# Input projection of a two-layer hybrid trunk: four of eight K pairs per chunk pair with seven block products, in two phases on four accumulators

## The chip, the cores and the metric

The kernel runs on one core of one Trainium2 chip. The metric is the device time of one execution in microseconds (us), the median of several runs. Engines are named as in the profile: PE (TensorE), DVE (VectorE), ACT (ScalarE), POOL (GpSimd), SP (SyncE, which here only issues DMAs).

## The reference

Two layers on x of 256 tokens by 2048 columns, in float32:

```python
for l in range(DEPTH):                                   # 2
    h = rms_norm(x, pre_mix_norm[l])
    proj = h @ w_in[l]                                   # 2048 x 6144
    # q_sb, k_sb, v_sb, q_d, k_d, v_d: six groups of 1024 columns, 8 heads each
    o_sb = rms_norm(stick_breaking_attention(q_sb, k_sb, v_sb), sb_out_norm[l])
    o_d = rms_norm(differential_attention(rope(q_d), rope(k_d), v_d, lam), diff_subln[l]) * (1 - lam_init)
    m = concat(o_sb, o_d) @ w_o[l]                       # 2048 x 2048
    x = x + rms_norm(m, post_mix_norm[l])
    h = rms_norm(x, pre_ffn_norm[l])
    x = x + rms_norm((silu(h @ w_gate[l]) * (h @ w_up[l])) @ w_down[l], post_ffn_norm[l])   # 5632 wide
```

## The kernel before

**Numbers.** A float32 matrix product is made of three matmuls. Each operand is split into `hi` (the value rounded to the PE's float32r format, made by ACT) and `lo` (the rest, made by DVE as value minus `hi`). `product` adds hi·hi, hi·lo and lo·hi into one PSUM accumulator of 128 tokens by 512 columns.

**Tiles.** K is taken in pairs of 128 rows ("K pair", eight of them for 2048), columns in chunks of 512, tokens in two halves. The twelve chunks of the input projection come in six pairs (`PAIRS`), numbered n = 0 to 5; four accumulators hold a chunk pair (2 token halves x 2 chunks). A plain K pair is eight products (`eight_in`): 2 rows of K x 2 token halves x 2 chunks.

**Seven products.** For some K pairs the 2x2x2 block product is done in Winograd's form with seven products (`seven_products`). The weight blocks of such a K pair are g (first chunk, rows 0 and 1) and u (second chunk, rows 0 and 1). Besides g0 and g1 the form needs five mixed blocks: t1, t2, t3, t4 and b22 (`mixed_weights`), and sums of token blocks (`pair_forms`, `token_sums`: `sh`, `sl`). Three or four of the seven products go to sums of their own (p1, p6, p7, q5), which are combined later (`shared_part`) and added when the accumulators are read.

**Input projection before** (`mixer_in`). Pair 0 is plain. In pairs 1 to 4, K pairs 4 and 5 have seven products, in the order `IN_ORDER`, with p1, p6, p7 and q5 in four extra PSUM banks; while these are taken, `burst` and `clear` keep attention out, which uses the same banks. After the second one `shared_part` reads the four banks (one ACT copy, four DVE operations), and `settle` adds the result to each of the four accumulators on DVE before ACT scales it. Pair 5 has no extra banks free: `sevens_alone` runs K pairs 4 and 5 first, in the four accumulators themselves, copies them out on ACT in between (`kept_part`), puts a plain K pair between, and three DVE operations combine the copies; `settle` then needs three additions (`added_alone`). The output projection starts with `sevens_alone` as well.

**Weights.** All weights lie in DRAM in the order in which they are used (`weight_order`, `weights_laid_out`), 512 KB a tile of two K rows by one chunk. `fetch` issues their loads on SP into four `raw` buffers, or for the sevens of this stage into four `late` rooms, shared with other stages (`GU`). The sum of the first row's blocks, t1, is made for most sevens of this stage by an accumulating DMA from POOL into SBUF (`added`). `feed` splits tiles in order into six `hi` and six `lo` buffers, four tiles ahead of the one in use (`LOOKAHEAD`); sevens hold their other mixed blocks in buffers of their own (`Th`, `Tl`).

**Attention.** It runs as generators beside the projection, moved on by `tick`, which is called once for each two products or so. A chunk pair's queries and keys are transposed (`flip`) some ticks behind the pair's end, 3 and 6 for the stick-breaking heads and 21 and 24 for the differential heads:

```python
            wait = 3
            for c in cc:
                if c // 2 not in (2, 5):
                    start(flip(c, toks), wait if c // 2 < 3 else wait + 18)
                    wait += 3
```

`diff_weights` then makes scores, softmax maps (`s_df`, `mx_df`, `e_df`) and their transposes, `stick_weights` the stick-breaking weights (`a_sb`, `ah_sb`), `attend` and `norm_pair` the heads' outputs. The order on each engine is fixed when the program is built.

Of the kernel before, what the change touches and what calls it, by code (L numbers as in the profile page):

```python
# [83 lines left out]
def in_order(n):  # L84

    if n == 0:
        return tuple(range(KT // 2))
    return IN_LAST if n == len(PAIRS) - 1 else IN_ORDER


def weight_order():
# [3 lines left out]
    def queue_pair(name, l, kp, c):  # L95
        order.append((name, l, kp, c))
        return len(order) - 1

    plan = []
    sevens, plain, own, added, aside = set(), set(), set(), set(), {}  # L100
    for l in range(L):
        lay = {"in": {}, "o": {}, "gate": {}, "up": {}, "down": {}}
        for n, (ca, cb) in enumerate(PAIRS):
            for kp in in_order(n):
                lay["in"][ca, kp] = queue_pair("w_in", l, kp, ca)
                lay["in"][cb, kp] = queue_pair("w_in", l, kp, cb)
                if kp in IN_NOW[n]:
                    plain.add(lay["in"][cb, kp])
                    if n > 1 or l:
                        added.add(lay["in"][cb, kp])  # L110
        aside[lay["in"][PAIRS[-1][1], IN_LAST[1]]] = "v"
        order_o = [(c, kp) for kp in KP_O for c in (0, 1)]
        order_o += [(c, kp) for kp in LATE_O for c in (2, 3)] + [(c, kp) for c in (2, 3) for kp in LAST_O]
        lay["order_o"] = order_o
        for c, kp in order_o:
# [3 lines left out]
            if c == 1 and kp in KP_O[:2]:  # L119
                plain.add(lay["o"][c, kp])  # L120
        aside[lay["o"][1, KP_O[1]]] = "sums"
# [16 lines left out]
    return order, plan, sevens, plain, own, added, aside  # L138


def weights_laid_out(inputs):

    import numpy as np

    order = weight_order()[0]
    out = np.empty((len(order), P, 2 * CW), np.float32)
    for o, (name, l, kp, c) in zip(out, order):
        w = inputs[name][l, kp * 2 * P : (kp + 1) * 2 * P, c * CW : (c + 1) * CW]
        o[...] = w.reshape(2, P, CW).transpose(1, 0, 2).reshape(P, 2 * CW)
    return out  # L150
# [36 lines left out]
def kernel(  # L187
# [35 lines left out]
    order, plan, sevens, plain, own, added, aside = weight_order()  # L223
# [8 lines left out]

    ready = {}
    raws, loads = [], []
    fed = [0]

    def fetch(upto):
        while len(raws) < min(upto, len(stream)):
# [7 lines left out]
            if i + 1 in sevens:  # L246
# [4 lines left out]
                continue  # L251
            if i in own or i + 1 in own:
                raw = mix_pool[0].tile([P, 2, CW], F32, tag="v", bufs=2, name=f"V{i}")
            elif i in plain or i + 1 in plain:
                raw = late_room([P, 2, CW], f"GU{i}")
            else:
                raw = wpool.tile([P, 2, CW], F32, tag="raw", bufs=4, name=f"raw{i}")
            mixing = bool({i, i + 1} & (own | plain))
            with not_ahead(i) if mixing else nullcontext():
                loads.append(nc.sync.dma_start(raw, stream[i]))  # L260
            raws.append(raw)
            if not mixing:
                usual.append((i, loads[-1]))
            elif i in added:
                nc.gpsimd.dma_start(raw[:, 0, :], stream[i - 1][:, 0, :], accum_op=ALU.add)
# [16 lines left out]
    heads_pool = [None]  # L282
    mix_raw = [None, 0, 0, 0]

    def mixed_weights(i):
# [4 lines left out]
        if i in own or i in aside:  # L290
            th = wpool.tile([P, 2, CW], F32R, tag="hi", bufs=6, name=f"Th{i}")
            tl = wpool.tile([P, 2, CW], F32R, tag="lo", bufs=6, name=f"Tl{i}")
        if i in own:
            th2 = mix_pool[0].tile([P, 2 * (S + P)], F32R, tag="ah", bufs=1, name=f"T2h{i}")[:, 0:CW]
            tl2 = mix_pool[0].tile([P, 2 * (S + P)], F32R, tag="al", bufs=1, name=f"T2l{i}")[:, 0:CW]
        elif i in aside:
            if aside[i] == "v":
                both = heads_pool[0].tile([P, 2, CW], F32R, tag="v", bufs=2, name=f"T2{i}")
                th2, tl2 = both[:, 0, :], both[:, 1, :]
            else:  # L300
                th2, tl2 = (
                    mix_pool[0].tile([P, 4, P], F32R, tag=tag, bufs=len(IN_SEVEN), name=f"T2{tag}{i}").rearrange("p j c -> p (j c)")
                    for tag in ("sh", "sl")
                )
        else:
            th = mix_pool[0].tile([P, 3, CW], F32R, tag="Th", bufs=1 if i in plain else 2, name=f"Th{i}")
# [1437 lines left out]
```

## Time and profile before

| | |
|---|---|
| median of 3 runs | 2175.76 us (2175.2 to 2175.97) |
| span of the profiled execution | 2174.5 us |
| PE busy, idle | 2161.7 us (99%), 12.8 us |
| DVE busy | 1941.0 us (89%) |
| ACT busy | 1413.9 us (65%) |
| granted TensorE clock | 1.000 |
| DMA | 475.16 MB, 219 GB/s |
| input projection, layer 0, pairs 0 to 5 end near | 47, 93, 142, 190, 240, 293 us |
| input projection, layer 1, pairs 0 to 5 end near | 1129, 1175, 1224, 1272, 1321, 1374 us |

The profile is of one execution, whose own time is its span; the median of the runs is 1.3 us longer. A line of a group has the line of kernel.py, the engine, the operation, what it writes and reads, shapes, the count, busy time and mean length, and the engine's idle time just before with what ended it. Matmul rows overlap: each is 0.39 us long, and the next one starts before it ends. The pairs' ends are read from the first reading of an accumulator behind each pair (the `w<-in,w` additions and the `tok` and `v` scalings).

### The profile page before, as it was taken

What the parts mean: (1) busy time and instruction counts of PE and PEld (TensorE: products, weight loads), DVE (VectorE), ACT (ScalarE), POOL (GpSimd) and SP (SyncE); (2) the same over time, 40 slices, a digit from 0 to 9 for tenths busy, and PEclk for the clock granted to TensorE, in tenths of its full rate; (3) what the DMA queues carried; (4) which work ended last, traced back from release to release, by engine and by line L of the source; (5) the groups of instructions that cost most, each with busy time, mean ns of one, the idle gap of its engine ahead of it and who ended that gap; (6) DMA issues with size and microseconds to landing.
All of it is one profiled execution on the core that took longest, in us unless ns stands there. A gap on an engine that the chain in (4) does not pass through costs nothing. (4 is left out here: it accounts for less than half of the span.)

```text
span 2174.5 us, 28797 instructions
## 1 busy us (share of the span) xinstructions
PE 2161.7 (99%) x9932; PEld 1781.1 (82%) x9932; DVE 1941.0 (89%) x2627; ACT 1413.9 (65%) x2113; POOL 261.7 (12%) x256
## 2 busy tenths in 40 slices
PE   9999999999999999999999999999999999999998
PEld 7888888888888888888888888888888888888886
DVE  7887878899999999999878888788999999999997
ACT  7666765765766666666566667757566666676664
POOL 1110000022221220000011100000212212200000
PEclk9999999999999999999999999999999999999999
DMA  9556446497887776777475564455978878767683
GB/s 331 188 184 219 161 170 202 156 305 235 245 259 225 232 234 224 234 226 256 149 252 184 198 207 166 165 184 182 293 237 255 253 226 237 234 214 246 202 269 99
DMA packets 142867, 475.16 MB, mean 219 GB/s; under 512 B 16240, under 2 KB 17264, under 8 KB 142208
## 3 DMA queue, kind: packets, MB, share of 16 engines
q1 hardware_dynamic: 121952, 436.03, 58.1%
q0 software_dynamic: 20192, 36.74, 10.1%
q8 instruction: 78, 1.28, 0.2%
q14 instruction: 69, 0.57, 0.1%
q10 hardware_dynamic: 576, 0.54, 0.1%
HBM read 464.86 MB, written 8.39 MB: 218 GB/s over the span
## 5 line engine op out<-in xcount | busy, mean ns | idle before, releaser
L349 DVE TENSOR_TENSOR lo<-raw,hi 128x1024 fp32r<-128x1024 f32 x442 | 535.3, 1230 | 77.8 <-ACT hi L339 77.0
L339 ACT ACTIVATE hi<-raw 128x1024 fp32r<-128x1024 f32 x464 | 475.1, 1056 | 74.6 <-PE in L1214 28.0
L1269 PE MATMUL c<-hi,xF 128*128 128x512 f32 x1344 | 364.4, 392 | 0.5 <-DVE xF L546 0.5
L1269 PEld LDWEIGHTS c<-hi,xF 128*128 128x128 f32 x1344 | 249.8, 188 | 53.0 <-ACT act L1479 1.6
L279 POOL DMA_DIRECT2D T<-in_weights_in_turn_dram x122 | 107.2, 879 | 1223.7 <-DMA T<-in_weights_in_turn_dram 311.9
L1269 PE MATMUL c<-lo,xF 128*128 128x512 f32 x672 | 207.4, 390 | 0.0
L311 ACT ACTIVATE Th<-T 128x512 fp32r<-128x512 f32 x122 | 77.2, 633 | 199.0 <-DVE T L322 196.0
L311 ACT ACTIVATE Th<-G 128x1024 fp32r<-128x1024 f32 x122 | 129.0, 1058 | 79.7 <-DVE G L323 78.3
L1592 PE MATMUL dn<-hi,jh 128*128 128x512 f32 x416 | 162.0, 389 | 0.0
L1593 PE MATMUL dn<-lo,jh 128*128 128x512 f32 x416 | 161.8, 389 | 0.0
L313 DVE TENSOR_TENSOR Tl<-G,Th 128x1024 fp32r<-128x1024 f32 x122 | 148.9, 1221 | 11.6 <-ACT Th L311 11.6
L339 ACT ACTIVATE hi<-G 128x1024 fp32r<-128x1024 f32 x122 | 128.8, 1056 | 36.6 <-DMA G<-in_weights_in_turn_dram 22.5
L313 DVE TENSOR_TENSOR lo<-T,hi 128x1024 fp32r<-128x1024 f32 x122 | 152.3, 1248 | 0.1
L323 DVE TENSOR_TENSOR G<-G,T 128x1024 f32<-128x1024 f32 x122 | 148.7, 1218 | 1.9
L1269 PEld LDWEIGHTS c<-lo,xF 128*128 128x128 f32 x672 | 126.0, 188 | 26.5
L349 DVE TENSOR_TENSOR lo<-G,hi 128x1024 fp32r<-128x1024 f32 x104 | 126.8, 1219 | 10.0 <-ACT hi L339 9.8
L311 ACT ACTIVATE hi<-T 128x1024 fp32r<-128x1024 f32 x122 | 128.0, 1049 | 11.3 <-PE c L1214 8.3
L1595 PE MATMUL dn<-hi,jl 128*128 128x512 f32 x416 | 128.1, 389 | 0.0
L1212 PE MATMUL in<-hi,xT 128*128 128x512 f32 x316 | 125.4, 398 | 0.7 <-ACT hi L948 0.7
L1213 PE MATMUL in<-lo,xT 128*128 128x512 f32 x316 | 123.1, 391 | 0.5 <-DVE lo L950 0.5
L1214 PE MATMUL in<-hi,xT 128*128 128x512 f32 x316 | 123.3, 391 | 0.0
L1212 PE MATMUL in<-hi,xI 128*128 128x512 f32 x292 | 116.5, 399 | 0.0
(532 smaller groups left out, 5040.5 us busy)
## 6 DMA issues: line engine op xcount, KB each, us to landing
raw<-in_weights_in_turn_dram SPq DMA_DIRECT2D x482, 512.0 KB, 4.9
T<-in_weights_in_turn_dram SPq DMA_DIRECT2D x122, 512.0 KB, 5.4
G<-in_weights_in_turn_dram SPq DMA_DIRECT2D x122, 512.0 KB, 5.4
T<-in_weights_in_turn_dram POOLq DMA_DIRECT2D x122, 256.0 KB, 5.7
GU<-in_weights_in_turn_dram SPq DMA_DIRECT2D x48, 512.0 KB, 6.0
GU<-in_weights_in_turn_dram POOLq DMA_DIRECT2D x18, 256.0 KB, 6.3
V<-in_weights_in_turn_dram SPq DMA_DIRECT2D x8, 512.0 KB, 5.7
away_ffn<-x SPq DMA_DIRECT2D x8, 512.0 KB, 7.2
```

The source lines that it names most:

```text
L311: nc.scalar.activation(h, w, AF.Copy)
L313: newest_rest[i] = nc.vector.tensor_tensor(out=l, in0=w, in1=h.bitcast(F32), op=ALU.subtract)
L323: nc.vector.tensor_tensor(out=g, in0=g, in1=t2.unsqueeze(1).to_broadcast([P, 2, CW]), op=ALU.add)
L339: nc.scalar.activation(hi, raw, AF.Copy)
L349: rest = nc.vector.tensor_tensor(out=lo, in0=raw, in1=hi.bitcast(F32), op=ALU.subtract)
L1212: nc.tensor.matmul(a, sh, hi, start=first, stop=False, skip_group_check=open_sums[0])
L1213: nc.tensor.matmul(a, sh, lo, start=False, stop=False, skip_group_check=open_sums[0])
L1214: return nc.tensor.matmul(a, sl, hi, start=False, stop=last, skip_group_check=open_sums[0])
L1269: nc.tensor.matmul(a, stat[part], w[j][:, kk, :], start=first and kk + n == 0, stop=last and kk == 1 and n == 2)
L1592: nc.tensor.matmul(accs[c, t], sh, hi[:, kk, :], start=first, stop=False, skip_group_check=open_sums[0])
L1593: nc.tensor.matmul(accs[c, t], sh, lo[:, kk, :], start=False, stop=False, skip_group_check=open_sums[0])
L1595: nc.tensor.matmul(accs[c, t], sl, hi[:, kk, :], start=False, stop=last, skip_group_check=open_sums[0])
```

## The change

In pairs 1 to 5 K pairs 0 to 3 have seven products, and K pairs 4 to 7 are plain and follow. All of these pairs use only the four accumulators, in two phases: first g0, t1, t2 and t3 of all four K pairs, then the four sums are copied out by ACT, then g1, b22 and t4 of all four go on in three of the same accumulators. The tiles are laid out by phase in DRAM; a tile of the first phase holds g0 and u0 of one K pair, one of the second holds g1 of two K pairs, and u1 of two K pairs is loaded into the `late` rooms. Splitting is counted in "jobs" of one `hi` and one `lo` tile: (g0, t1), (t2, t3), (g1, g1), (b22, t4). The sum t1 is made in DRAM one chunk pair ahead: SP copies u0 to a scratch tensor, POOL accumulates g0 onto it, and the load takes it as the tile's second half; pair 1 of layer 0 has no such time ahead and adds on DVE. Pair 0 makes four sets of token sums, not two. `burst` and `clear` are gone. The output projection's two sevens go through the same new function without a plain unit between them.

```diff
-IN_SEVEN = (4, 5)
-IN_ORDER = (0, 1, 4, 2, 5, 3, 6, 7)
-IN_LAST = (4, 5, 0, 1, 2, 3, 6, 7)
-IN_NOW = ((), IN_SEVEN, IN_SEVEN, IN_SEVEN, IN_SEVEN, IN_SEVEN)
-SETTLE = 2
+IN_SEVEN = (0, 1, 2, 3)
+IN_PLAIN = (4, 5, 6, 7)
...
+    def queue_phase(key, name, l, kps, cc):
+        for a, b in zip(kps[::2], kps[1::2]):
+            roles[queue(*((name, l, 2 * kp + 1, cc[1]) for kp in (a, b)))] = "u1", key, (a, b)
+            for kp in (a, b):
+                roles[queue(*((name, l, 2 * kp, c) for c in cc))] = "first", key, (kp,)
+        for a, b in zip(kps[::2], kps[1::2]):
+            roles[queue(*((name, l, 2 * kp + 1, cc[0]) for kp in (a, b)))] = "g1", key, (a, b)
...
+            if i in first_sums:
+                for j, src in enumerate((stream[i][:, 0, :], first_sums[i])):
+                    loads.append(nc.sync.dma_start(raw[:, j, :], src))
...
+    def sums_ahead(key):
+        mine = [i for i, role in roles.items() if role[:2] == ("first", key)]
+        total = {}
+        for i in mine:
+            total[i] = kept.tile([P, CW], F32, name=f"sum{i}")
+            with in_turn():
+                nc.sync.dma_start(total[i], stream[i][:, 1, :])
+            yield
+        for i in mine:
+            nc.gpsimd.dma_start(total[i], stream[i][:, 0, :], accum_op=ALU.add)
+            first_sums[i] = total[i]
+            yield
...
+    def first_part(i, n, key, kp):
+        raw, u1 = raws[i], kept_u1[key, kp]
+        hi, lo = split_tile(f"{i}_{n}")
+        if n == 0:
+            if i not in first_sums:
+                nc.vector.tensor_tensor(out=raw[:, 1, :], in0=raw[:, 0, :], in1=raw[:, 1, :], op=ALU.add)
+            nc.scalar.activation(hi, raw, AF.Copy)
+            nc.vector.tensor_tensor(out=u1[:, 1, :], in0=u1[:, 0, :], in1=raw[:, 1, :], op=ALU.subtract)
+            rest_of(lo, raw, hi)
+            names = "g0", "t1"
+        else:
+            nc.vector.tensor_tensor(out=raw[:, 1, :], in0=raw[:, 0, :], in1=u1[:, 1, :], op=ALU.add)
+            for j, src in enumerate((u1[:, 1, :], raw[:, 1, :])):
+                nc.scalar.activation(hi[:, j, :], src, AF.Copy)
+                rest_of(lo[:, j, :], src, hi[:, j, :])
+            names = "t2", "t3"
...
+    def second_part(i, n, key, kps):
+        raw = raws[i]
+        hi, lo = split_tile(f"{i}_{n}")
+        if n == 0:
+            for j, kp in enumerate(kps):
+                t2 = kept_u1[key, kp][:, 1, :]
+                nc.vector.tensor_tensor(out=t2, in0=raw[:, j, :], in1=t2, op=ALU.add)
+            src = raw
+        else:
+            src = kept_u1[key, kps[n - 1]]
+        nc.scalar.activation(hi, src, AF.Copy)
+        rest_of(lo, src, hi)
...
+                if n + 1 < len(PAIRS):
+                    start(sums_ahead(("in", l, n + 1)))
+                else:
+                    start(sums_ahead(("o", l)))
+                if n:
...
+                    phased(banks, forms, xT, ("in", l, n), IN_SEVEN, w)
...
+    def phased(banks, sums, tiles, key, kps, w):
+        x11, x12, x21, x22 = banks
...
+        def products(kp, *names):
+            feed_jobs(job + 6 + next(n for n, left in enumerate(unread) if left))
...
+        a, b, z = kps[0], kps[1], kps[-1]
+        products(a, "g0", "t1")
+        if len(kps) > 2:
+            products(b, "g0", "t1")
+        products(a, "t2", "t3")
+        if len(kps) > 2:
+            products(b, "t2", "t3")
+        for kp in kps[2:-1]:
+            products(kp, "g0", "t1")
+            products(kp, "t2", "t3")
+        products(z, "t2")
+        kept_part(1, x22)
+        products(z, "g0")
         kept_part(0, x11)
+        products(z, "t1")
         kept_part(3, x12)
+        products(z, "t3")
         kept_part(2, x21)
         p1, p6, p7, q5 = w
         nc.vector.tensor_tensor(out=p6, in0=p6, in1=p1, op=ALU.subtract)
         nc.vector.tensor_tensor(out=q5, in0=q5, in1=p1, op=ALU.subtract)
         nc.vector.tensor_tensor(out=q5, in0=q5, in1=p7, op=ALU.subtract)
+        for kp, after in zip(kps[::2], kps[1::2]):
+            products(kp, "g1")
+            products(after, "g1")
+            products(kp, "b22", "t4")
+            products(after, "b22", "t4")
```

More of the change, by code (lines that the diff above doesn't have):

```diff
@@ L137, in weight_order @@
         plan.append(lay)
-    return order, plan, sevens, plain, own, added, aside
+    return order, plan, sevens, own, roles
 def weights_laid_out(inputs):
@@ L231 @@
     newest_seven = [None]
+    jobs = []
+    jobs_to = []
+    for i in range(len(order)):
+        parts = {"u1": 0, "first": 2, "g1": 3}[roles[i][0]] if i in roles else 1
+        jobs += [(i, n) for n in range(parts)]
+        jobs_to.append(len(jobs))
     ready = {}
+    blocks, kept_u1, first_sums = {}, {}, {}
     raws, loads = [], []
@@ L313, in split @@
                 newest_rest[i] = nc.vector.tensor_tensor(out=l, in0=w, in1=h.bitcast(F32), op=ALU.subtract)
-        if (i in plain or i in own) and i not in added:
+        if i in own:
             with after_rests():
@@ L344, in feed @@
                     tc.add_manual_dep(rest.ins, newest_seven[0].ins.name, AFTER, reason="the shared port")
-                ready[i] = (hi, lo)
-                fed[0] += 1
                 continue
-            with behind():
-                rest = nc.vector.tensor_tensor(out=lo, in0=raw, in1=hi.bitcast(F32), op=ALU.subtract)
-            ready[i] = (hi, lo)
-            fed[0] += 1
-            rests.append(rest)
+            rest_of(lo, raw, hi)
     def rounded_next():
-        i = fed[0]
+        i = jobs[fed[0]][0]
         fetch(i + 1)
@@ L1189, in added_alone @@
         return to
-    def seven_in(banks, extra, sums, xT, l, cc, kp, first, last):
-        hi, lo = weights(plan[l]["in"][cc[0], kp], LOOKAHEAD)
-        m = weights(plan[l]["in"][cc[1], kp], LOOKAHEAD)
-        seven_products(banks, extra, sums, *pair_blocks(xT, kp), hi, lo, m, first, last)
     def pair_blocks(tiles, kp):
```

233 lines of the change are left out of this document (102 added, 131 removed).

## The prediction

> **What bounds the kernel now.** I read the head of the page first, then the engines' busy time by stretch (one row per chunk pair of the first layer's input projection), then single rows of the order of time for the pace of TensorE and VectorE.
>
> ```profile
> span 2174.5 us, 28797 instructions
> PE 2161.7 (99%) x9932; PEld 1781.1 (82%) x9932; DVE 1941.0 (89%) x2627; ACT 1413.9 (65%) x2113; POOL 261.7 (12%) x256
> ...
> 56.78 0.39 PE L1214 MATMUL in<-hi,xT 128*128 128x512 f32 x1
> ...
> 62.00 0.39 PE L1213 MATMUL p_in<-lo,xT 128*128 128x512 f32 x1
> ```
>
> The two matmul rows are the first and last of 24 in a row: 5.22 us over 23 steps, so one 512-wide matmul costs 0.227 us of TensorE's path, not the 0.39 us of its row (they overlap). A product (three matmuls: hi·hi, hi·lo, lo·hi) is 0.68 us. TensorE has 13 us of idle time in the whole span, so a product left out is worth 0.68 us, as long as nothing else becomes late.
>
> ```profile
> 47.00:93.00 46.00, 46.00 (x222) 37.95 (x222) 33.42 (x44) 25.63 (x31) 12.53 (x18) 1.00 0.70 241
> 93.00:142.00 49.00, 48.71 (x234) 39.59 (x233) 41.39 (x70) 32.11 (x72) 5.59 (x10) 1.00 0.56 184
> 142.00:190.00 48.00, 48.00 (x242) 39.66 (x241) 35.58 (x46) 29.93 (x55) 7.86 (x10) 1.00 0.58 189
> 190.00:240.00 50.00, 50.00 (x244) 40.82 (x243) 43.54 (x72) 34.30 (x69) 1.72 (x2) 1.00 0.52 158
> 240.00:293.00 53.00, 53.00 (x266) 44.58 (x265) 42.56 (x65) 39.66 (x67) 0.00 (x0) 1.00 0.46 159
> 1175.00:1224.00 49.00, 48.72 (x235) 39.58 (x234) 41.38 (x70) 32.11 (x72) 5.58 (x10) 1.00 0.53 175
> ```
>
> Columns: length, then busy time of PE, weight load, DVE, ACT, POOL, the granted clock, DMA share. The first five rows are chunk pairs 1 to 5 of layer 0 (pair 0 has no seven-product work), the sixth is pair 2 of layer 1, which repeats the first layer's to 0.01 us; so I work with one layer and double. TensorE is full; VectorE is second, at 41.39 of 49 us in pair 2. Two kinds of pair show: 2 and 4 carry the softmax of the differential heads (41 to 44 us of DVE), 1 and 3 little of it.
>
> **What VectorE pays per block.**
>
> ```profile
> 795.00 1.22 DVE L323 TENSOR_TENSOR G<-G,T 128x1024 f32<-128x1024 f32 x1
> 796.14 0.68 DVE L313 TENSOR_TENSOR Tl<-T,Th 128x512 fp32r<-128x512 f32 x1
> 796.74 0.68 DVE L322 TENSOR_TENSOR T<-T 128x512 f32<-128x512 f32 x1
> 797.34 1.22 DVE L349 TENSOR_TENSOR lo<-raw,hi 128x1024 fp32r<-128x1024 f32 x1
> L349 DVE TENSOR_TENSOR lo<-raw,hi 128x1024 fp32r<-128x1024 f32 x442 | 535.3, 1230 | 77.8 <-ACT hi L339 77.0
> ```
>
> Start to start, a 1024-wide operation takes 1.14 us and a 512-wide one 0.60 us. A plain K pair costs two `lo` operations, 2.28 us of DVE for 5.44 us of PE (8 products). A seven-product K pair before: four wide and two narrow, 5.76 us for 4.76 us of PE. After: five narrow single steps (u1 minus t1, t3, two rests of t2 and t3, t2 into t4) and 2.5 wide rests, 5.85 us. So a chunk pair goes from 2 x 5.76 + 6 x 2.28 = 25.2 to 4 x 5.85 + 4 x 2.28 = 32.5 us, +7.3; pairs 1 to 4 save two PSUM operations (four shared-part and four settling ones become three and three, some 1.3 us), so +6.0 there. Pair 2 then needs 41.4 + 6.0 = 47.4 us of DVE in 49.0 - 1.4 = 47.6 us. On average that fits; the question is the order.
>
> **The change part by part.**
>
> TensorE: two more seven-product K pairs in 5 chunk pairs of 2 layers, one product each: 20 x 0.68 = 13.6 us less. This is the whole gain.
>
> The order inside a pair: before, the two sevens stand among plain K pairs (0, 1, 4, 2, 5, 3, ...). After, 28 seven-products (19.0 us of PE) come first and 32 plain ones (21.8 us) follow. The seven stretch needs 4 x 5.85 = 23.4 us of DVE. The hi and lo buffers are six each; at the start of a pair two still hold the last plain K pair, so at most four tiles are ready: the first-phase tiles of two K pairs, 2 x 3.54 = 7.1 us of DVE done ahead, worth 8 products or 5.4 us of PE. Within the 19.0 us the DVE must then do 23.4 - 7.1 = 16.3, the three differences of the kept sums (1.8), the settling of the pair before (two reads of PSUM, 1.3) and the two plain tiles that come next (2.3): 21.7 us, 2.7 us late with no attention in it. Three microseconds of that can slip: the 1.8 of differences behind the plain tiles, and two u1 subtractions (1.2) ahead of their buffers. So a pair without attention waits 0 to 2.7 us, against 1.36 saved.
>
> Attention in the first 22 us of pairs 2 and 4, tile `e_df` and then tile `s_df` (columns of the first fence of stretches, without POOL):
>
> ```profile
> 93.00:115.00 22.00, 0.00 (x0) 0.00 (x0) 3.39 (x12) 5.15 (x24) 1.00 0.30 103
> 190.00:212.00 22.00, 0.00 (x0) 0.00 (x0) 3.58 (x12) 3.09 (x15) 1.00 0.53 160
> ...
> 93.00:115.00 22.00, 1.37 (x8) 0.94 (x8) 2.80 (x7) 5.15 (x24) 1.00 0.30 103
> 190.00:212.00 22.00, 1.14 (x8) 0.69 (x8) 1.57 (x4) 3.09 (x15) 1.00 0.53 160
> ```
>
> DVE 3.39 + 2.80 = 6.2 us against 1.4 of PE in pair 2, 5.2 against 1.1 in pair 4: another 4.8 and 4.1 us late. It stays there: the flips start 21 and 24 ticks behind a pair's end as before, and a pair shrinks only from 32 to 30 ticks. Pair 2 waits 4.5 to 7.5 us, pair 4 3.8 to 6.8. What the plain stretch has left cannot be brought forward, since six buffers end the lead. Afterwards the plain tiles cost 2.28 per 5.44 us and PE runs full again.
>
> I take a third of the way from the low end (the order on DVE above is fine-grained, so most of what can slip will): 5.5, 4.8 and 0.9 for each of pairs 1, 3, 5; 13.0 us a layer, 26 in all.
>
> The Trainium skill says the same in general ("Perfetto Trace Analysis", Optimization Strategy): where a kernel has regimes with different limiting engines, interleaving them can help. This change separates them; by that rule alone it loses. The rows agree so far as before, interleaved, shows a full PE with DVE at 41 of 49.
>
> Copies out of the accumulators between the phases, on ACT:
>
> ```profile
> L1165 ACT COPY w<-in 128x512 f32<-128x512 f32 x8 | 4.4, 599 | 0.0
> ```
>
> The split of a tile on ACT, from the page's groups:
>
> ```profile
> L339 ACT ACTIVATE hi<-raw 128x1024 fp32r<-128x1024 f32 x464 | 475.1, 1056 | 74.6 <-PE in L1214 28.0
> ```
>
> Pair 5 already had the copies in the same banks, and shows 53.00 of 53.00 us busy. After, two products (1.36 us) stand between the sum's end in x11 and the next write to it; copy plus one split ahead of it on ACT (0.60 + 1.06) is 1.66. Bounds 0 and 0.3 us a pair; I take 0.1, 1 us in all. The Trainium skill's advice ("Perfetto Trace Analysis", Matmuls: rotate independent groups through different PSUM banks) speaks against reusing the four banks here; by it the upper end would be the one, 3 us in all.
>
> Sums made ahead in DRAM: per pair four copies (SP) and four accumulations (POOL), 256 KB each, in place of two accumulations into SBUF; issued a pair ahead, eight steps at two ticks.
>
> ```profile
> GU<-in_weights_in_turn_dram POOLq DMA_DIRECT2D x18, 256.0 KB, 6.3
> q0 software_dynamic: 20192, 36.74, 10.1%
> ```
>
> Landing takes 6.3 us for the nearest kind; with a copy before it, some 13 us against some 20 us of lead (13 of a pair's 30 ticks in 47 us). DMA is at 0.46 to 0.70 in these stretches, and 1.5 MB more traffic in 47 us is 32 GB/s on 160 to 240. The second block's halves load into four late rooms, each freed by its second-phase split, a plain stretch before SP needs it again; POOL has nothing else in a pair but the rotations. Cost 0; without that cover the first load of a pair waits on SP with all later loads behind it, at most the 6.3 us, once a pair. I keep that out of the likeliest.
> Pair 1 of layer 0 has no such sums: four additions on DVE, two of them behind the lead, 1.2 us.
>
> Four instead of two sets of token sums in pair 0: two more a layer, each two operations of 0.42, four of 0.28 and one of 0.68 us.
>
> ```profile
> L1004 DVE TENSOR_TENSOR fin<-xI 128x256 f32<-128x256 f32 x4 | 1.6, 413 | 0.0
> L1219 DVE TENSOR_TENSOR sin<-fin 128x128 f32<-128x128 f32 x4 | 1.1, 282 | 0.0
> L1230 DVE TENSOR_TENSOR slin<-sin,shin 128x512 fp32r<-128x512 f32 x4 | 2.7, 684 | 0.6 <-ACT shin L1229 0.6
> 1102.00:1115.00 13.00, 12.45 (x63) 10.16 (x63) 13.00 (x35) 11.02 (x29) 0.00 (x0) 1.00 0.86 299
> 1115.00:1129.00 14.00, 14.00 (x64) 11.59 (x63) 10.54 (x23) 8.84 (x16) 0.00 (x0) 1.00 0.88 305
> ```
>
> That is 5.3 us of DVE where layer 1 leaves 3.5 us idle (14.00 - 10.54): 0 to 1.8 a layer; I take 0.5, 1 us in all, the slack being nearly enough. The output projection's two sevens take 11.7 us of DVE after, 11.5 + 1.2 before (its sums come ready now): 0, bounds -1 and +1.5 a layer, since the plain unit between its sevens is gone.
>
> Sum against the profiled 2174.5 us: -13.6 + 26 + 1 + 1.2 + 1 = +15.6, 2190. The median of the runs, 2175.76, lies 1.3 us above that span; I state 2191.
>
> **The rivals.**
> (a) The cover holds, and the change is faster. For it: the gate/up stage has four sevens in a row with the same 23 us of DVE to 19 of PE, and runs full at full DVE:
>
> ```profile
> 820.00:862.00 42.00, 42.00 (x191) 34.89 (x190) 41.86 (x48) 30.71 (x37) 0.88 (x1) 1.00 0.58 189
> ```
>
> Against it: a tile there gives more lead. Two sevens ahead are 9.5 us of PE, here four tiles are 5.4, and there is no softmax. It decides if the wait per pair stays below 1.36 us on average: 2175.8 - 13.6 + 1 = 2163.
> (b) All that can slip does: 4.5 + 3.8 + 3 x 0 = 8.3 a layer, 16.6 - 13.6 and 1 for the rest: 2180, no measurable change.
> (c) ACT and DVE hold each other up. In a seven stretch ACT has four times 1.06 + 1.3 + 0.5 + 1.06 us and four copies, 18 of 19 us, with 5.2 us of exponentials in pair 2 and 3.1 in pair 4 (the ACT column above) beside it. Then the upper ends come: 7.5 + 6.8 + 3 x 2.7 = 22.4 a layer, and 3 + 1.2 + 3.6 + 3 for the rest: 2217.
>
> **How the numbers follow.** A difference below 0.2% (4.4 us) can hardly be told from none here. Chances: likeliest case 0.45, (a) 0.25, (b) 0.18, (c) 0.12. Slower: 0.45 + 0.12 and a fifth of (b), 0.60; same 0.15; faster 0.25, all of (a). The range must reach into both signs: 2163 holds most of (a), 2209 leaves out most of (c). The likeliest case alone: 2182 to 2200.
>
> **What would show it.** Right: TensorE waits for `lo` rows of DVE (or `hi` of ACT) in the first 20 us of pairs 2 and 4, and DVE is full there, while in the second half of each pair DVE idles with ACT waiting for PE to free buffers; 60 matmuls fewer; pair 2 at 51 to 54 us in place of 49, pair 3 near 47. Wrong: if the pairs are all 1.4 us shorter and PE waits nowhere, the lead is deeper than four tiles, or the order on DVE puts the softmax behind the tiles; if the waits name DMA, the sums in DRAM came late.

## The result, and the profile after

The changed kernel takes 2202.12 us (2199.45 to 2204.53), the kernel before in the same session 2175.86 us: a ratio of 1.0119, 95% interval 1.0105 to 1.0134. It is slower by 26 us, on the side that was forecast, 11 us above the forecast 2191 and inside its range, 2163 to 2209.

Head of the page of the kernel after (as before: busy time, share, instructions):

```profile
span 2201.6 us, 29139 instructions
PE   2162.3 (98%) x9872; PEld 1770.4 (80%) x9872; DVE 2011.8 (91%) x2783; ACT 1461.4 (66%) x2203; POOL 300.8 (14%) x278
```

TensorE has the 60 matmuls fewer and VectorE 70.8 us more. The stretches that answer to those of before, one row per chunk pair, 1 to 5 of layer 0 and then of layer 1; columns as in the prediction, with PE, weight load, DVE, ACT, POOL, granted clock, DMA share and GB/s:

```profile
48.60:96.50 47.90, 46.37 (x205) 35.92 (x205) 41.54 (x57) 31.75 (x42) 15.53 (x21) 1.00 0.75 237
96.50:152.00 55.50, 52.34 (x254) 40.50 (x254) 50.07 (x86) 39.66 (x95) 11.10 (x13) 1.00 0.72 211
152.00:201.40 49.40, 46.25 (x220) 36.68 (x219) 42.45 (x56) 31.22 (x48) 9.48 (x12) 1.00 0.64 203
201.40:253.90 52.50, 51.71 (x258) 41.74 (x257) 50.58 (x89) 43.86 (x90) 3.37 (x4) 1.00 0.70 204
253.90:303.50 49.60, 49.60 (x245) 41.58 (x244) 46.34 (x71) 39.86 (x66) 0.00 (x0) 1.00 0.48 162
1143.10:1197.30 54.20, 43.31 (x188) 34.54 (x187) 39.58 (x48) 30.11 (x41) 32.85 (x22) 0.91 0.73 222
1197.30:1251.00 53.70, 51.88 (x261) 40.97 (x260) 47.40 (x84) 39.46 (x94) 7.72 (x12) 1.00 0.69 201
1251.00:1301.30 50.30, 46.30 (x221) 36.72 (x220) 42.57 (x57) 31.31 (x48) 8.97 (x12) 1.00 0.64 196
```

Read the first three columns against each other: the PE column now falls short of the length in pairs 1, 2 and 3 (in pair 1 of layer 1 by 11 us, with the clock at 0.91 and POOL at 32.85 us), while pairs 4 and 5 are full or nearly so. The counts say something else: pair 4 has 258 matmul records where it had 244, although the change takes six away, and pair 5 has 245 where it had 266 (242 and 258 with the kernel before divided as in the table below). Attention work has moved from pair 5 (and the stage behind it) into pair 4. A pair's length alone is therefore no measure of what it waited.

Lengths from ScalarE's first scaling behind one pair (`tok` or `v`) to its first scaling behind the next, in us, for the kernels told of below. In the kernel before, an addition on VectorE stands some 0.8 us ahead of this scaling behind pairs 1 to 4; counted from the first reading of an accumulator its pairs 1 and 5 are some 45.9 and 52.5 us long, the others the same within 0.2:

| pair | before | after | e7 | e10 | e12 |
|---|---|---|---|---|---|
| layer 0: 1, 2 | 46.7, 48.7 | 47.9, 55.4 | 47.7, 54.1 | 46.7, 48.7 | 46.6, 51.3 |
| 3, 4, 5 | 48.2, 49.2, 51.7 | 49.5, 52.5, 49.6 | 45.4, 52.4, 49.6 | 44.7, 51.8, 49.6 | 45.7, 52.8, 49.7 |
| o to pair 0 of layer 1 | 836.9 | 839.6 | 836.0 | 835.7 | 835.3 |
| layer 1: 1, 2 | 46.7, 48.7 | 54.1, 53.8 | 44.3, 55.2 | 43.1, 53.9 | 45.4, 50.6 |
| 3, 4, 5 | 48.5, 49.0, 51.7 | 50.3, 52.5, 49.6 | 45.9, 52.2, 49.6 | 44.4, 51.8, 49.6 | 45.5, 52.8, 49.7 |

The list of what TensorE waited for in the kernel after (us in total, times, longest):

```profile
PE qkT_ps L1119 <- POOL tok L968: 10.2, 1, 10.2
PE oT_ps_df L800 <- DVE on_df L786: 5.3, 4, 1.7
PE in L1266 <- DVE lo L352: 4.8, 12, 0.7
PE in L1265 <- DVE w L1244: 3.3, 2, 2.1
...
PE in L1265 <- ACT hi L388: 1.7, 1, 1.7
PE in L1265 <- ACT w L1203: 1.5, 2, 0.9
```

The forecast `lo` waits are there, with `on_df` and `w` also on a late VectorE. The largest was not forecast: one wait of 10.2 us for a rotation on GpSimd. The order of time around it, GpSimd first, then VectorE's first and last instruction of the stretch, then TensorE:

```profile
1143.89 21.85 POOL L965 TENSOR_TENSOR ra<-tok,rope_sb 128x128 f32<-128x128 f32 x1 [0.30 <-ACT tok L1101]
1165.71 0.31 POOL L966 TENSOR_TENSOR rb<-tok,rope_sb 128x64 f32<-128x64 f32 x1
...
1166.90 0.45 POOL L965 TENSOR_TENSOR ra<-tok,rope_sb 128x128 f32<-128x128 f32 x1
...
1143.68 1.82 DVE L352 TENSOR_TENSOR lo<-raw,hi 128x512 fp32r<-128x512 f32 x2
...
1164.74 0.69 DVE L1235 TENSOR_TENSOR w<-w 128x512 f32<-128x512 f32 x1
...
1156.25 0.39 PE L1267 MATMUL in<-hi,slin 128*128 128x512 f32 x1
1166.88 0.90 PE L1119 MATMUL qkT_ps<-ident,tok 128*128 128x128 f32 x3 [10.24 <-POOL tok L968]
...
1168.43 0.63 PE L1267 MATMUL in<-hi,xI 128*128 128x512 f32 x1
1168.86 0.63 PE L1265 MATMUL in<-hi,xI 128*128 128x512 f32 x1
```

```profile
1143.70:1165.40 21.70, 12.29 (x51) 8.96 (x49) 21.70 (x29) 14.93 (x22) 21.51 (x1) 0.88 0.69 220
1165.40:1166.90 1.50, 0.02 (x1) 0.02 (x1) 0.03 (x1) 0.00 (x0) 1.35 (x4) 0.50 0.00 0
```

The same `ra` takes 0.45 us at 1166.90 and 21.85 us at 1143.89. In these 21.7 us VectorE is busy 21.70, without a pause; `ra` ends 0.3 us behind the end of that run. VectorE stopped only because TensorE stood (since 1156.6) and freed no buffers: its next instruction waits 6.04 us for ScalarE's `hi`, and that `hi` 8.73 us for TensorE. Behind the wait the clock is at half, and matmuls start 0.43 us apart instead of 0.227.

A third thing is late at the head of pair 3. VectorE, then SP, in the order of time of the kernel after:

```profile
147.90 0.48 DVE L805 SCALAR_TENSOR_TENSOR mix_df<-oT_ps_df,gains,mix_df 128x256 fp32r<-128x256 f32 x1 [0.54 <-ACT mix_df L802]
153.75 0.69 DVE L382 TENSOR_TENSOR u<-raw,u 128x512 f32<-128x512 f32 x1 [5.37 <-DMA raw<-in_weights_in_turn_dram]
...
146.99 0.33 SPq L277 DMA_DIRECT2D raw<-in_weights_in_turn_dram  x1
147.38 1.25 SPq L288 DMA_DIRECT2D sum<-in_weights_in_turn_dram  x1
```

VectorE stands 5.37 us in front of one g1 tile, issued at 146.99, with everything else on VectorE behind it in the fixed order: a full engine that idles.

### The profile page after: what moved, and what is told of

Same layout as the page of the kernel before. It is cut to its first block, busy times and chain, and to the rows that moved or that the text cites. A ratio compares the mean times of both kernels' runs of the same rounds, so it can differ in the third digit from the quotient of the medians.

```text
span 2201.6 us, 29139 instructions
## 1 busy us (share of the span) xinstructions
PE 2162.3 (98%) x9872; PEld 1770.4 (80%) x9872; DVE 2011.8 (91%) x2783; ACT 1461.4 (66%) x2203; POOL 300.8 (14%) x278
## 4 chain that ended last, share of the span: by engine, by line
PE 83%; DVE 8%; DMA 4%; ACT 2%; issue 2%; POOL 1%; DVEq 0%; SPq 0%; ACTq 0%; POOLq 0%
PE c L1322 20%; PE dn L1641 4%; PE dn L1642 4%; PE dn L1644 4%; DVE lo L352 4%; PE in L1265 4%; PE in L1267 4%; PE in L1266 4%; DMA raw<-in_weights_in_turn_dram 3%; PE p L1266 3%; PE c L1266 3%; PE c L1265 3%; PE p L1267 3%; PE c L1267 3%; PE p L1265 3%; PE o L702 2%
## 5 line engine op out<-in xcount | busy, mean ns | idle before, releaser
L352 DVE TENSOR_TENSOR lo<-raw,hi 128x1024 fp32r<-128x1024 f32 x512 | 597.4, 1184 | 56.8 <-ACT hi L414 47.7
L414 ACT ACTIVATE hi<-raw 128x1024 fp32r<-128x1024 f32 x424 | 435.5, 1057 | 98.2 <-DMA raw<-in_weights_in_turn_dram 64.9
L1265 PE MATMUL in<-hi,xT 128*128 128x512 f32 x284 | 112.6, 401 | 2.5 <-ACT w L1203 1.5
L1266 PE MATMUL in<-lo,xT 128*128 128x512 f32 x284 | 111.6, 394 | 0.4 <-DVE lo L352 0.4
L1267 PE MATMUL in<-hi,xT 128*128 128x512 f32 x284 | 111.3, 393 | 0.0
L1266 PE MATMUL in<-lo,xI 128*128 128x512 f32 x260 | 102.9, 396 | 2.4 <-DVE lo L352 2.4
```

The costliest lines, as they stand in the source:

```text
L352: rests.append(nc.vector.tensor_tensor(out=lo, in0=src, in1=hi.bitcast(F32), op=ALU.subtract))
L414: nc.scalar.activation(hi, raw, AF.Copy)
L1265: nc.tensor.matmul(a, sh, hi, start=first, stop=False, skip_group_check=open_sums[0])
L1266: nc.tensor.matmul(a, sh, lo, start=False, stop=False, skip_group_check=open_sums[0])
L1267: return nc.tensor.matmul(a, sl, hi, start=False, stop=last, skip_group_check=open_sums[0])
```

## The experiments

Three theories of the 26 us, and a fourth for the whole. **D**: VectorE cannot keep up in the seven stretch with the short lead that six buffers give (the prediction's own). **P**: GpSimd's rotations are held up by a VectorE that never pauses, and the transposes wait for them. **S**: the sums in DRAM load the DMA engines and queues, and push tiles back. **O**: the order itself, all sevens ahead of all plain K pairs. Ratios are against the kernel before in the same session, whose median was 2175.0 to 2176.2.

**e1: two plain K pairs between the phases.** `between` takes a plain K pair, 4 and then 5, ahead of each half of the second phase, in the order of tiles and of products.

```diff
-        for kp, after in zip(kps[::2], kps[1::2]):
+        for m, (kp, after) in enumerate(zip(kps[::2], kps[1::2])):
+            if between:
+                between(m)
...
             products(kp, "g1")
```

> Theory D (VectorE cannot make the tiles of four seven-product K pairs in a row as fast as TensorE uses them, and the lead is four tiles): two of the four plain K pairs now stand between the second phase's halves, same work on every engine. First phase needs 14.2 - 7.1 + 1.3 + 2.3 = 10.7 us of VectorE in 10.9 us of TensorE, so the light pairs stop waiting and the softmax pairs keep 2 to 4 us: 2175 to 2188 us, against 2202. Rival P (the loss is the rotations on POOL, held up by a VectorE without pauses, and the half clock behind that wait): 2190 to 2202, since the first phase keeps VectorE full. Rival S (sums made in DRAM come late): 2199 to 2205, no change.

Measured: 2190.59 us, ratio 1.0065 (1.0047 to 1.0083), 11.5 us less than the kernel after with the same work. So O and D hold a good part, though the time lies above D's range and at the low end of P's. P's wait has not gone; GpSimd's rows of this kernel, and one of VectorE:

```profile
1140.56 0.82 POOL L296 DMA_DIRECT2D sum<-in_weights_in_turn_dram  x1 [16.34 <-DVE lo L357]
1141.11 27.49 POOL L970 TENSOR_TENSOR ra<-tok,rope_sb 128x128 f32<-128x128 f32 x1
...
1173.56 0.81 POOL L296 DMA_DIRECT2D sum<-in_weights_in_turn_dram  x1
...
1187.53 0.69 DVE L368 TENSOR_TENSOR u<-u,raw 128x512 f32<-128x512 f32 x1 [6.18 <-DMA raw<-sum]
```

VectorE's unbroken run is longer here, and `ra` with it, 27.49 us. TensorE waits 4.8 us for this rotation, not 10.2. But GpSimd issues the accumulations of the sums in the same fixed order, and three of the four for pair 2 of layer 1 now stand behind `ra` and the rotations that follow it. VectorE then waits 11.8 us, three times, for sums between 1177 and 1191 us, and pair 2 takes 57.2 us. So a held rotation can make the sums late as well: P and S are not independent. (In the kernel after the same accumulations queue behind `ra`, but VectorE waits only 0.6 us for them there.)

**e2: no sums in DRAM.** The copies and accumulations are left out, and u0 is loaded where the sum would be; so t1 is another weight, and the output another.

```diff
-            total[i] = kept.tile([P, CW], F32, name=f"sum{i}")
-            with in_turn():
-                nc.sync.dma_start(total[i], stream[i][:, 1, :])
             yield
         for i in mine:
-            nc.gpsimd.dma_start(total[i], stream[i][:, 0, :], accum_op=ALU.add)
-            first_sums[i] = total[i]
+            first_sums[i] = stream[i][:, 1, :]
```

> Leaves out the making of the weight sums: no copies into DRAM and no accumulations by POOL; the second half of a first-phase tile is loaded straight from the stream, so t1 is u0 alone and later numbers differ. All work of VectorE, ScalarE and TensorE stays. Rival S: the loss goes, 2165 to 2190. Theory D: 2199 to 2205, as no engine of the chain has less to do. Rival P: 2199 to 2205 too, since the rotation that ran 21.9 us began when its input was ready, and not late behind an accumulation.

Measured: 2189.71 us, ratio 1.0061 (1.0046 to 1.0076), again some 12 us less, at the upper edge of S's range. S holds. At the head of pair 3:

```profile
147.77 0.69 DVE L378 TENSOR_TENSOR u<-raw,u 128x512 f32<-128x512 f32 x1 [2.00 <-DMA raw<-in_weights_in_turn_dram]
```

The same g1 tile is issued at 144.38 and there 3.4 us later; with the sums it took 6.8 us from its issue. VectorE stands 2.00 us, not 5.37, and pair 3 is 4 us shorter in both layers. `ra` is at 21.85 us as before: P is not S.

**e3: the rotations on VectorE.**

```diff
-        eng = nc.gpsimd
+        eng = nc.vector
```

> The 32 rotation operations a layer move from POOL to VectorE (some 0.2 to 0.3 us each, 6 to 9 us a layer, most in pairs 1 to 3). Rival P: the 10.2 us wait of the first transposes of layer 1 and the slow matmuls behind it go: 2187 to 2191. Theory D: that single wait goes as well, but the other waits grow by a part of what is added: 2191 to 2200, with pairs 2 and 3 of each layer longer than in the changed kernel.

Measured: 2189.33 us, ratio 1.0062 (1.0046 to 1.0079), 13 us less although VectorE has more to do. Pair 1 of layer 1 falls from 54.1 to 44.2 us, and TensorE's wait for the rotation and the half clock behind it are gone from that pair. Pairs 3 are 2.4 and 2.0 us shorter too, which P does not explain.

**e4: two sevens in the new order.** The form of the change, with the number of sevens of the kernel before.

```diff
-IN_SEVEN = (0, 1, 2, 3)
-IN_PLAIN = (4, 5, 6, 7)
+IN_SEVEN = (0, 1)
+IN_PLAIN = (2, 3, 4, 5, 6, 7)
```

> Two of eight K pairs with seven products in the same two phases on four accumulators (K pairs 0 and 1 seven, 2 to 7 plain): TensorE's work is that of the kernel before. Theory D: with two, the stretch needs 11.7 - 7.1 + 1.8 + 1.3 + 2.3 = 10.0 us of VectorE in 9.5 us, and the plain tiles behind give 3.2 us back per K pair: 2174 to 2184. Rival O (phasing itself costs it: copies out of the banks in use, sums in DRAM, no banks of their own): the waits stay and the saving of 13.6 us goes, 2205 to 2216.

Measured: 2181.69 us, ratio 1.0026 (1.0016 to 1.0036). With a seven stretch of half the length the two-phase form costs 5.5 us over the kernel before at equal TensorE work: inside D's range, and far from what O expected. The groups of `ra` in the kernel before, in the kernel after, and here (16 each; busy time, mean ns):

```profile
L901 POOL TENSOR_TENSOR ra<-tok,rope_sb 128x128 f32<-128x128 f32 x16 | 11.3, 704 | 42.4 <-ACT tok L1042 28.6 <-DMA lams<-in_lambda_q_dram 13.3
```

```profile
L965 POOL TENSOR_TENSOR ra<-tok,rope_sb 128x128 f32<-128x128 f32 x16 | 33.4, 2089 | 21.4 <-ACT tok L1101 20.9
```

```profile
L965 POOL TENSOR_TENSOR ra<-tok,rope_sb 128x128 f32<-128x128 f32 x16 | 13.2, 827 | 50.5 <-ACT tok L1101 29.9 <-DMA lams<-in_lambda_k_dram 20.2
```

In the middle one 21.85 of the 33.4 us are a single instruction. The short stretch leaves VectorE pauses (0.65 and 0.29 us around the first rotations of pair 1 in layer 1), and there `ra` takes 0.78 to 1.40 us.

Pauses are not the whole of it. A stretch of pair 1 of layer 0 in the kernel after, columns as before:

```profile
52.60:61.20 8.60, 8.03 (x35) 5.87 (x34) 8.60 (x11) 4.04 (x7) 8.21 (x11) 1.00 0.54 185
```

VectorE is busy for 8.60 of 8.60 us with two-input operations, and GpSimd gets its rotation operations done beside it, each in 0.76 to 1.32 us, while VectorE's 512-wide operations start 0.69 to 0.87 us apart instead of 0.60. So P as it was put, that a VectorE without pauses holds GpSimd, is too strong. The long hold shows in three kernels (after, e1, e2), each time at the first rotation of pair 1 of layer 1, and each time it ends 0.3 us behind VectorE's run. What sets this rotation apart from those that are let in is not shown.

**e5: e3 and e1 together.**

> The rotations of the heads on VectorE, and two plain K pairs placed between the two phases of the sevens. Alone the first gave -12.8 us, the second -11.5 against the changed kernel. P (the held GpSimd) and D (too short a lead ahead of VectorE) together: the two remove different waits, so they add but for the 10 us that both lose in pair 1 of layer 1; 2175 to 2183, pair 1 of layer 1 at 44 to 45 us, pair 3 still near 50 for the late tile. If one cause stood behind both gains (they overlap): 2187 to 2190. S (the sums in DRAM): the 8 to 12 us of the sums stay, so it cannot fall below 2175.

Measured: 2177.04 us, ratio 1.0005 (0.9995 to 1.0014). Rotations and order add up, 13 and 12 us: P and O/D are two causes. Pairs 3 are at 45.3 and 45.7 us, against the expectation: with plain work between the phases the late g1 tile is hidden (VectorE waits 0.9 us for g1 tiles in all, where it waited 11.5 us for two of them in the kernel after).

**e6: the rotations on VectorE in the kernel before.** The control for e3, with the same edit.

> The kernel before with the rotations of the heads on VectorE in place of GpSimd, all else as before. P (GpSimd is held only where VectorE runs without a pause for 20 us, which only the change brings): nothing to gain here, some 1.6 us more of VectorE a head pair: 2174 to 2179. Rival (moving the rotations is a gain of its own, whatever the order of the sevens): 2160 to 2168, the 12.8 us that the same edit gave to the changed kernel.

Measured: 2175.86 us, ratio 1.0001 (0.9992 to 1.0010). The move gains nothing by itself; the 13 us of e3 belong to what the change does to GpSimd.

**e7: e3 and e2 together.** The output is another, as in e2.

> The changed kernel with the rotations on VectorE and without the sums in DRAM: the first weight of each K pair is loaded where its sum would be, so the output is another. If the GpSimd term (-12.8) and the sums' term (-12.4) are separate, as P and S together say: 2175 to 2179, pairs 1 and 3 near 45 to 47 us, and what is left against the kernel before is D's, in pairs 2 and 4 alone (52 to 55 us). If both edits only relieved the same moment, pair 1 of layer 1: 2184 to 2189.

Measured: 2183.77 us, ratio 1.0039 (1.0024 to 1.0054): 18.3 us less than the kernel after, not the 25.2 of e2 and e3 added. P's and S's terms overlap by some 7 us, nearer to the second expectation than to the first. Pair 1 of layer 1 is at 44.3 us and pairs 3 at 45.4 and 45.9; what is left of the loss lies in pairs 1 and 2 of layer 0 and pair 2 of layer 1. The head of pair 2 of layer 0 in e7, columns as before:

```profile
95.00:100.00 5.00, 5.00 (x24) 4.15 (x23) 5.00 (x10) 2.56 (x4) 0.00 (x0) 1.00 0.33 106
100.00:105.00 5.00, 5.00 (x23) 3.77 (x22) 5.00 (x14) 4.83 (x8) 0.00 (x0) 1.00 0.33 105
105.00:110.00 5.00, 5.00 (x22) 3.69 (x21) 5.00 (x8) 2.78 (x4) 0.00 (x0) 1.00 0.30 105
110.00:115.00 5.00, 3.47 (x15) 2.56 (x15) 4.99 (x13) 3.33 (x6) 0.00 (x0) 1.00 0.74 256
115.00:120.00 5.00, 3.31 (x18) 2.62 (x17) 4.98 (x9) 4.10 (x12) 0.00 (x0) 1.00 0.26 75
```

This is D as the prediction drew it: VectorE full from the first microsecond, TensorE short for the first time 15 us in, when the lead is used up. The waits of the same pair, TensorE's first, then ScalarE's between 95 and 120 us:

```profile
PE in L1261 <- ACT hi L384: 1.7, 1, 1.7
PE in L1261 <- ACT w L1199: 1.5, 1, 1.5
```

```profile
ACT hi L365 <- DVE raw L363: 4.5, 2, 2.3
```

TensorE's waits name ScalarE, but ScalarE had itself waited 4.5 us for VectorE's `raw`: follow a wait one step back before its engine is blamed.

**e8: e7 without the scaling and combining of the softmax maps.** These VectorE operations are left out, so the maps are another result too.

```diff
-            for i in range(len(hs)):
-                nc.vector.tensor_scalar_mul(e[0][:, i, :], e[0][:, i, :], sm[:, 0, i : i + 1])
-                nc.vector.scalar_tensor_tensor(
-                    out=e[0][:, i, :], in0=e[1][:, i, :], scalar=sm[:, 1, i : i + 1], in1=e[0][:, i, :], op0=ALU.mult, op1=ALU.add
-                )
```

> As the run before it, and on VectorE the scaling and combining of the two softmax maps left out as well (16 operations in each of pairs 2 and 4 of a layer, some 3.4 us of VectorE a pair), so the output is another. D (VectorE is full in the first 20 us of pairs 2 and 4, each microsecond less there is a microsecond of the end): 3 to 4 us less in each of four pairs, 12 to 16 us below the run before it, 2160 to 2166. Rival (TensorE waits there for buffers or ScalarE, or VectorE's idle second half takes the work up anyway): less than 4 us below it.

Measured: 2177.41 us, ratio 1.0008 (0.9998 to 1.0018), 6.4 us below e7, between both expectations. Pair 2 is 2.3 us shorter in both layers, pair 4 only 0.5 and 0.3. So VectorE's work in the stretch counts in pair 2, at about 0.7 us for one. The pairs account for the 6.4 us only in part: in this profile pair 3 of layer 1 is 2.1 us longer, with a wait of 4.40 us for its g1 tile (3.17 in e7), and the two profiled spans differ by 3.6 us. Pair 4 does not wait for that work, though it is 3 us longer than before: that is the attention work moved there.

**e9: one pause of VectorE behind each rotation.** The rotations stay on GpSimd.

```diff
         eng.tensor_tensor(out=v16, in0=ra, in1=rb, op=ALU.add)
+        nc.vector.tensor_copy(out=ra[:, 0, 0:1], in_=tok[:, 0:1])
```

> The changed kernel with the rotations left on GpSimd, and behind each of them one copy of a single column on VectorE that reads the rotated tile; so VectorE stops until GpSimd is done with it. P (GpSimd gets nowhere while VectorE runs without a stop, and one stop frees it): `ra` back to 0.5 to 2 us, the 10 us wait of the transposes and the half clock gone, pair 1 of layer 1 at 45 to 48 us instead of 54.1; VectorE pays one to two us for each of some six rotations a layer that fall into a full stretch; 2189 to 2197. Rival (the rotation is slow for a reason of its own, as a cold GpSimd or its input): `ra` stays at 20 us, VectorE now stands still behind it, and the end is at 2205 to 2225.

Measured: 2213.80 us, ratio 1.0175 (1.0159 to 1.0191). For this rotation the mechanism is P's, since a stop of VectorE ends the hold: the same `ra` takes 1.54 us and the transposes' wait for GpSimd is gone from TensorE's list. Pair 1 of layer 1 falls to 50.3 us, not to the 45 to 48 expected, and the end lies in the rival's range: the pauses cost more than P put down for them. GpSimd's row, and VectorE's wait over the whole run:

```profile
1150.73 1.54 POOL L965 TENSOR_TENSOR ra<-tok,rope_sb 128x128 f32<-128x128 f32 x1
```

```profile
DVE ra L969 <- POOL tok L968: 29.4, 16, 4.3
```

VectorE stands 29.4 us in 16 pauses. In e3 the rotations run on VectorE itself, which takes some 12.4 us (its busy time in e6 against the kernel before), and the end of e9 comes 24 us later than that of e3. That is more than the 17 us between the two, so not all of it is VectorE's time; where the rest lies is not shown.

**e10: e5 without the sums in DRAM** (the output is another, as in e2).

> Rotations on VectorE, two plain K pairs between the phases, and no sums in DRAM: the first weight is loaded in place of the sum, so the output is another. D, P and S together: the run with the first two edits (2177) less the 4 to 8 us that the sums still cost beside them, 2168 to 2173; the ideal of a full TensorE is 2162. S wrong beside a lead (with plain work in between, the late tiles are hidden anyway): 2175 to 2178.

Measured: 2167.52 us, ratio 0.9962 (0.9948 to 0.9976), 7.7 us faster than the kernel before. The stretches of pairs 1 to 4 of layer 0:

```profile
47.20:93.80 46.60, 46.60 (x216) 36.88 (x215) 44.76 (x78) 33.15 (x50) 0.00 (x0) 1.00 0.60 205
93.80:142.60 48.80, 48.80 (x244) 39.94 (x243) 48.37 (x93) 37.73 (x82) 0.00 (x0) 1.00 0.49 164
142.60:187.30 44.70, 44.70 (x218) 36.81 (x217) 42.30 (x66) 31.93 (x57) 0.00 (x0) 1.00 0.59 198
187.30:239.00 51.70, 51.65 (x258) 42.04 (x257) 49.08 (x87) 43.53 (x89) 0.00 (x0) 1.00 0.50 163
```

TensorE is full in all of them again, with VectorE at 48.37 of 48.80 us in pair 2. With the three causes gone 7.7 of the 13.6 us of saved products show. Full by this column is not yet the fastest pace, since the rows of matmuls overlap: PE's busy time falls from 2161.7 to 2152.2 us, 9.5 and not 13.6. In layer 1 pair 1 takes 43.1 and pair 2 53.9 us, with 197 and 263 matmul records where the kernel before has 225 and 235: attention work has moved there too.

**e11: e5 with the sums made in SBUF.** Instead of the copies, GpSimd's queue accumulates g0 onto the loaded tile, as the kernel before does.

```diff
-                for j, src in enumerate((stream[i][:, 0, :], first_sums[i])):
-                    loads.append(nc.sync.dma_start(raw[:, j, :], src))
+                loads.append(nc.sync.dma_start(raw, stream[i]))
+                nc.gpsimd.dma_start(raw[:, 1, :], stream[i][:, 0, :], accum_op=ALU.add)
...
```

> The same two edits, and each pair's weight sum accumulated by GpSimd's queue into the tile in SBUF right behind its load, as the kernel before has it for its two sevens; no copies in DRAM, nothing left out. S in its first form (the 256 KB copies in DRAM load the DMA engines and push other tiles back): 2169 to 2174, faster than the kernel before. Rival (the accumulation's landing behind the load is what is late, wherever the sum is made): 2176 to 2184.

Measured: 2219.47 us, ratio 1.0206 (1.0191 to 1.0221), 42 us above e5: worse than either expectation. VectorE's wait:

```profile
DVE u L364 <- DMA raw<-in_weights_in_turn_dram: 50.2, 16, 7.3
```

Load and accumulation, one behind the other, now stand ahead of each tile. Making the sums a pair ahead in DRAM is the better of the two; S is right that they cost, not that SBUF would be the cure.

**e12: e5 with the sums on VectorE.** No copies; `first_part` adds in every pair, as in pair 1 of layer 0. Nothing is left out.

> Rotations on VectorE, two plain K pairs between the phases, and the weight sums by VectorE itself, one addition of 0.60 us for each seven-product K pair, in all later pairs as pair 1 of layer 0 has it; no sums in DRAM, nothing left out. Against the run with no sums at all (2167.5) VectorE has four more additions in eight pairs, 19 us. D with the rate that leaving out the maps showed (6.4 us of the end for 13.6 us of VectorE): half of it comes back, 2174 to 2179, no better than the sums in DRAM (2177). Rival (between the phases the plain K pairs leave VectorE room for the additions, and the late landings were the worse): 2168 to 2172, and faster than the kernel before.

Measured: 2174.08 us, ratio 0.9996 (0.9987 to 1.0005). Against e10, 19 us of additions cost 6.6 us, at the low edge of D's range. It is the best complete version here, no faster than the kernel before by this measurement. The 13.6 us that four sevens save on TensorE are lost again to VectorE's work.

## Why the prediction was right, and where it was not

The direction was right, and so was the mechanism that was put first, a VectorE that comes too late in the seven stretch. That the total came out 11 us from the forecast is luck: the term for VectorE was some 8 us too large, and 18.3 us of P and S stood in no term.

- **TensorE's saving, 13.6 us.** 60 matmuls fewer, and 7.7 us net in e10, where TensorE is full.
- **VectorE's work per pair.** Right: +31.3 us a layer was the sum over the five pairs; the stretches give 231.0 - 196.5 = 34.5 in layer 0, the four additions of pair 1 (2.4) in it.
- **VectorE's lateness, 26 us: too large.** e7, without the two causes that the sum does not have (and with the rotations on VectorE), comes nearest to what that sum describes: +15.6 was forecast, +7.7 measured, so the term with its small companions is some 21 us, not 29; rival (b), with +4, was nearer. The step that failed is pair 4: a wait of 4.8 us was taken, but its rows show TensorE at 51.71 of 52.50 us, and e8 gains 0.3 to 0.5 there. It grew by 3.3 us because attention came forward out of pair 5, which shrank by 2.1; the output projection shrank too, from 54.9 to 52.9 us, against a forecast of 0. The flips did stay where they were in ticks, but the attention that follows on them moved. The place was off as well. In the first 20 us VectorE is full, as forecast (from 96 us 19.95 of 20 us in pair 2, from 201 us 19.97 in pair 4), but TensorE's rows are short of only 0.9 and 0.6 us there; most of what pair 2 loses comes later, 33.71 busy of 36 us.
- **Pairs 1, 3, 5 and 2.** Pair 2 was put at 51 to 54 (55.4 and 53.8), pair 3 near 47 (49.5 and 50.3; without the sums in DRAM 45.4 and 46.5).
- **The sums in DRAM, 0: wrong.** They cost 12 us in the kernel after and 9.5 beside e5's edits (e5 against e10). The bound of 6.3 us once a pair was there, and was kept out of the likeliest because landing times left 7 us of room. In the kernel after the sums themselves are seldom late (VectorE waits 6.1 us for them, in six waits; in e1 17.3 us in 13). What was overlooked is that the copies delay other tiles, as the g1 tile above, and that a late tile stops everything behind it on VectorE. Ahead of pair 1 of layer 1 the DMA engines are also busy throughout (share 1.03, of the kernel after):

```profile
1115.00:1129.30 14.30, 14.30 (x66) 11.85 (x65) 12.25 (x39) 10.57 (x26) 3.22 (x4) 1.00 1.03 309
```

Before, the share was 0.88 there, in a row that the prediction used for VectorE alone.
- **GpSimd: not seen.** "POOL has nothing else in a pair but the rotations" counted its instructions, not who waits for them, nor what it would hold up in turn. 13 us (e3, with e6 as its control). The long hold shows in one pair of ten only, where e3 gains 9.9 of these 13 us: in pair 1 of layer 0 GpSimd begins while VectorE has pauses (1.96 us busy of 48.0 to 52.6), and its later rotations get through beside a full VectorE.
- **Copies on ScalarE, 1 us:** `w` 1.5 us in two waits. **Token sums, 1 us:** not tested alone; in e7 and e10 the stretch that holds pair 0 of layer 1 is about 1 us shorter than before, with 2 us gained in the output projection in it, which agrees.
- **The order.** The Trainium skill's rule from "Perfetto Trace Analysis", Optimization Strategy, that interleaving stages with different limits may gain, was set against the change in the prediction. Two plain K pairs between the phases give 11.5 us (after to e1), 12.3 (e3 to e5) and 16.3 (e7 to e10): the trace agrees three times.

Still open: the 6 us between e10 and the ideal 2162; why one rotation was held over a whole run of VectorE and the others were not; and whether more `hi` and `lo` buffers would do what the order does, which was not tried. P and S overlap by 7 us. One link is shown, the accumulations that queue behind a held rotation (e1). By pairs, some 4 us of the overlap lie in pairs 3, which e2 shortens by 4.1 and 3.8 us, e3 by 2.4 and 2.0, and e7, with both edits, by 4.1 and 4.4; why e3 shortens them is open.

## What to carry to other kernels

Before work is shifted to an engine that is second to the bound, look for what other engines do in its pauses: if VectorE loses them, check in the trace whether GpSimd's operations grow, who waits for them, and what GpSimd still has to issue behind them. Place the stretches in which the second engine is the limit between those in which it has room, and then count transfers that move earlier as work on the queue that issues them. And compare kernels whose work can move between stages by the sum over the stages, not stage by stage.

## What the hardware showed that was not expected

A GpSimd operation of 0.45 us took 21.85 us in one kernel and 27.49 in another beside a VectorE that ran two-input operations without a pause (29 instructions in 21.7 us), and ended 0.3 us behind the end of that run. The Trainium skill ("SBUF — State Buffer", Who interferes with whom) says that a VectorE instruction with two SBUF inputs and a GpSimd instruction that reads SBUF contend, that the ports they share are an exclusive lock, and that the order of issue decides who is blocked. From 52.6 to 61.2 us the trace agrees: the two engines' instructions pass one another, each a little longer. In the long hold GpSimd was not let in between two VectorE instructions either, over the whole run of them, and a pause of VectorE (e9) brought the same instruction back to 1.54 us. That it is this port is the page's reading; the runs show that a pause ended the hold, not why it began.

The wait of 10.2 us cost more than itself: the granted clock is at 0.50 from 1160.3 to 1170.5 us, so the seven steps from the first 512-wide matmul behind the wait, at 1167.43, take 3.13 us where they would take 1.59 at 0.227 us each, another 1.5 us.
